# Attention scores of the token-order units in two full-height passes, with the units in another order

## The chip, the cores and the metric

The kernel runs on one core of one Trainium2 chip. The time is the device time of one launch in microseconds (us). The kernel before took 852.31 us, the median of 3 runs (850.77 to 853.92). A core has engines that each work through a queue of their own in order and wait for each other by semaphores: TensorE (PE: matrix products and transposes; weight loads are shown apart as PEld), VectorE (DVE), ScalarE (ACT), GpSimd (POOL) and SyncE (SP), which issues the DMAs here.

## The reference

One layer with 512 tokens, model width 1024, heads of 64. All inputs are float32.

```
hn   = rms_norm(x, ln_g);  proj = hn @ w_in
A    = block-sparse causal attention, 8 heads (with 512 tokens: causal over all keys)
B    = three groups of 8 heads, (window, dilation) = (128,1), (512,4), (2048,16),
       outputs mixed by their softmax denominators
C    = sliding window of 128, 8 query heads on 2 key heads, learned sinks
       (all: per-head rms_norm of q and k, relative-position bias, softmax)
br   = [A * silu(ga), B * silu(gb), C * silu(gc)] @ w_branch   (per branch)
out  = x + (sum over branches of sigmoid(gates) * br) @ w_out
```

## The kernel before, in words

A float32 value v is kept as two tiles, hi (v rounded to the type fp32r) and lo = v - hi. A product of two such values is written as three matmuls that add into one PSUM tile: hi·hi, hi·lo, lo·hi. The normalised input is held transposed as `xhi`, `xlo`.

**Units.** The attention work is cut into ten units, each half (4 heads) of one kind. Kind A is mixer A. Kinds W, R, Z are the three groups of mixer B. Kind C is mixer C. A, W and C work on the tokens in their order (`natural_attention`). R and Z work on residue classes of the token number modulo 4 (`residue_attention`). The order is A0 W0 R0 Z0 A1 W1 R1 Z1 C0 C1.

**Projection** (`project`). Per unit and per 128-token tile t, 24 matmuls (8 slices of the contraction, three passes) make 512 columns of q and k in the PSUM tile `pj`, and 24 more make 256 columns of v. Then per tile: ACT copies q and k to `qn` and squares them, DVE sums, POOL takes the power -1/2, DVE multiplies, PE transposes two head pairs of q and two of k (L420), ACT writes the hi part with the norm's gain and DVE the lo part (L430, L431). Two heads share a tile: the first in partitions 0 to 63, the second in 64 to 127. `qn` comes from a pool tag of 3 buffers.

**Scores** (`natural_attention`). For A and W a head's score of one query tile is made by `mm3` (L436, L437, L438) from 64 partitions: qhi·khi, qhi·klo, qlo·khi. Its width is 256 columns, for A 384 and 512 in the last two query tiles. For C the queries are already stacked: `stack_queries` (L342 to L349) makes for each head a tile with the hi part in partitions 0 to 63 and the lo part in 64 to 127, and the keys stand twice, so that L471 on 128 partitions gives (qhi + qlo)·khi and L472 on 64 partitions gives qhi·klo. Behind the scores: DVE adds the bias and takes the row minimum (L447), ACT takes the exponential (L448, with a read of the accumulator), PE transposes (L485), ACT and DVE write hi and lo of the transposed probabilities (`pthi`, `ptlo`), PE multiplies by v (L510). The residue units have their own loop: scores in plain float32 on 64 partitions (L535), transposes (L546), PV products by `mm3`, and copies of the result (L563).

**End of a unit** (`spread`). Per-row factors are brought to all 64 channels of a head by a product with a 0/1 matrix `emat` from 64 partitions (tile `pb`, L590).

**What sets the order.** The program is written unit by unit, and a scheduler then sets a fixed order on each engine by its own timing model, within the limits of data, buffers and explicit `issue_after` edges. `RATION` names the units during whose attention the next unit's projection is handed out piece by piece (A0, W0, W1, C0, C1). Elsewhere the scheduler may still pull projections of the next unit into an attention, as far as their buffers are free. The tags of q and k (`qhi`, `qlo`, `khi`, `klo`) have two buffers each. After the attention come gates, branch products and the output projection.

## Time and profile before

| | |
|---|---|
| median of 3 runs | 852.31 us (850.77 to 853.92) |
| the profiled execution, its own time | 849.95 us |
| its span, first to last instruction | 848.2 us |
| PE, PEld, DVE, ACT, POOL busy | 97%, 78%, 51%, 49%, 20% |
| mean granted TensorE clock | 0.989 |

The profile is that of one execution. The end of a matmul is modelled and overlaps the next one, so that busy shares of PE run high: the distance from one start to the next is the better price of a matmul. A matmul of 512 columns is shown as 128x512, and the partitions it contracts over stand ahead as 128*128 (contracted * output).

### The profile page before, as it was taken

How to read it: one execution, taken by the hardware profiler on the slowest of the kernel's cores; microseconds unless marked ns; L12 is line 12 of the kernel's file. 1: busy time of each engine (PE TensorE's matmuls, PEld its weight loads, DVE VectorE, ACT ScalarE, POOL GpSimd, SP SyncE). 2: the span in 40 equal slices, each digit the busy share in tenths (PEclk: the TensorE clock that was granted, in tenths of full speed). 3: DMA queues.
4: the chain of work that ended last, by engine and by line, in shares of the span. 5: the costliest groups of instructions: out<-in, count | busy, mean ns of one | idle time of the engine just before them, and what ended most of it. 6: DMA issues, size and time to landing. Idle time of an engine off the chain costs nothing.

```text
span 848.2 us, 11663 instructions
## 1 busy us (share of the span) xinstructions
PE 823.3 (97%) x4295; PEld 664.4 (78%) x4295; DVE 429.1 (51%) x981; ACT 412.8 (49%) x913; POOL 170.1 (20%) x113
## 2 busy tenths in 40 slices
PE   7999999999998999989999899999999999999998
PEld 5888887788877688868787777777888888888886
DVE  6746553645465567245555485645243733332612
ACT  5535553748577356256576845654344333222310
POOL 4333011122212321111131160103131310110200
PEclk9999999999999999999999899999999999999999
DMA  8445233251332042413332121503432431531302
GB/s 267 135 128 139 63 100 106 68 169 43 95 106 76 22 134 84 147 58 100 118 105 80 39 57 38 146 23 99 150 100 76 148 100 51 198 100 50 124 1 100
DMA packets 60605, 83.57 MB, mean 99 GB/s; under 512 B 4835, under 2 KB 40803, under 8 KB 60548
## 3 DMA queue, kind: packets, MB, share of 16 engines
q1 hardware_dynamic: 60548, 82.83, 31.4%
q8 instruction: 34, 0.56, 0.3%
q14 instruction: 23, 0.19, 0.1%
HBM read 74.36 MB, written 8.45 MB: 98 GB/s over the span
## 4 chain that ended last, share of the span: by engine, by line
PE 88%; ACT 5%; DVE 3%; issue 1%; DMA 1%; POOL 1%; DVEq 0%; SPq 0%; POOLq 0%; ACTq 0%
PE pj L363 12%; PE pj L364 11%; PE pj L365 11%; PE pj L266 8%; PE pj L268 8%; PE pj L267 8%; PE acc L856 5%; PE po L510 4%; PE tr L485 3%; PE po L830 3%; PE po L831 3%; PE po L832 3%; PE sc L436 2%; ACT lg L448 2%; PE tr L420 2%
## 5 line engine op out<-in xcount | busy, mean ns | idle before, releaser
L363 PE MATMUL pj<-whi,xhi 128*128 128x512 f32 (+1 forms) x576 | 204.0, 354 | 1.3 <-ACT xhi L130 0.7
L364 PE MATMUL pj<-wlo,xhi 128*128 128x512 f32 (+1 forms) x576 | 198.0, 344 | 0.0
L365 PE MATMUL pj<-whi,xlo 128*128 128x512 f32 (+1 forms) x576 | 196.6, 341 | 0.0
L135 DVE TENSOR_TENSOR wlo<-w,whi 128x1024 fp32r<-128x1024 f32 x82 | 109.1, 1338 | 113.6 <-ACT whi L130 112.7
L130 ACT CAST whi<-w 128x1024 fp32r<-128x1024 f32 x108 | 112.9, 1051 | 61.7 <-PE po L831 31.6
L135 POOL TENSOR_TENSOR wlo<-w,whi 128x1024 fp32r<-128x1024 f32 x28 | 68.1, 2432 | 309.7 <-ACT whi L130 309.6
L363 PEld LDWEIGHTS pj<-whi,xhi 128*128 128x128 f32 x576 | 109.5, 190 | 19.0 <-issue 2.5
L365 PEld LDWEIGHTS pj<-whi,xlo 128*128 128x128 f32 x576 | 109.2, 190 | 13.4 <-issue 1.3
L364 PEld LDWEIGHTS pj<-wlo,xhi 128*128 128x128 f32 x576 | 109.5, 190 | 12.1 <-issue 1.0
L266 PE MATMUL pj<-xhi,whi 128*128 128x512 f32 x288 | 115.4, 401 | 0.0
L268 PE MATMUL pj<-xhi,wlo 128*128 128x512 f32 x288 | 114.2, 397 | 0.0
L267 PE MATMUL pj<-xlo,whi 128*128 128x512 f32 x288 | 113.6, 394 | 0.0
L141 POOL TENSOR_TENSOR rr<-rv,mhalf 128x8 f32<-128x8 f32 (+2 forms) x40 | 65.1, 1629 | 231.2 <-DVE rv L139 216.7
L130 ACT CAST pthi<-tr 128x128 fp32r<-128x128 f32 (+3 forms) x112 | 44.2, 399 | 42.7 <-PE tr L485 37.5
L268 PEld LDWEIGHTS pj<-xhi,wlo 128*128 128x128 f32 x288 | 54.4, 189 | 12.0 <-issue 0.5
L266 PEld LDWEIGHTS pj<-xhi,whi 128*128 128x128 f32 x288 | 54.5, 189 | 11.6 <-issue 0.2
L267 PEld LDWEIGHTS pj<-xlo,whi 128*128 128x128 f32 x288 | 54.5, 189 | 11.3 <-issue 0.2
L135 DVE TENSOR_TENSOR ptlo<-tr,pthi 128x128 fp32r<-128x128 f32 (+3 forms) x112 | 50.8, 458 | 22.5 <-ACT pthi L130 20.2
L447 DVE CUSTOM_DVE_ANT_0 lg<-sc,bt 128x128 f32<-128x128 f32 (+3 forms) x128 | 41.9, 361 | 39.1 <-PE tr L485 29.5
L379 DVE TENSOR_REDUCE ss<-sq 128x8 f32<-128x512 f32 (+2 forms) x40 | 25.7, 643 | 47.9 <-ACT sq L377 47.5
L448 ACT ACTIVATE lg<-lg,sm 128x128 f32<-128x128 f32 (+1 forms) x96 | 40.2, 420 | 15.4 <-DVE sm L447 15.2
L448 ACT ACTIVATE lg<-lg,sl 128x128 f32<-128x128 f32 (+2 forms) x64 | 33.5, 523 | 26.9 <-DVE sl L447 26.6
(178 smaller groups left out, 1252.6 us busy)
## 6 DMA issues: line engine op xcount, KB each, us to landing
w<-in_w_in SPq DMA_DIRECT2D x54, 512.0 KB, 4.1
w<-in_w_in SPq DMA_DIRECT2D x72, 256.0 KB, 3.1
w<-in_w_branch SPq DMA_DIRECT2D x12, 512.0 KB, 3.4
vscr<-vn SPq DMA_DIRECT2D x16, 256.0 KB, 2.6
w<-in_w_out SPq DMA_DIRECT2D x8, 512.0 KB, 4.5
xt<-in_x SPq DMA_DIRECT2D x4, 512.0 KB, 6.5
bt<-scr SPq DMA_DIRECT2D x8, 256.0 KB, 3.1
bt<-scr SPq DMA_DIRECT2D x16, 128.0 KB, 3.0
```

The costliest lines, as they stand in the source:

```text
L130: A.copy(dst, src)
L135: eng.tensor_tensor(dst, src, hi.bitcast(F32), ALU.subtract)
L141: G.tensor_tensor(r, v, mhalf[:, :n], ALU.pow)
L266: T.matmul(psum, a, xhi[:, k, :], start=(k == 0), stop=False)
L267: T.matmul(psum, a, xlo[:, k, :], start=False, stop=False)
L268: T.matmul(psum, wlo(k)[:, c : c + 128], xhi[:, k, :], start=False, stop=(k == KT - 1))
L363: T.matmul(pj[:, :ncol], xh, whi(k), start=(k == 0), stop=False)
L364: T.matmul(pj[:, :ncol], xh, wlo(k), start=False, stop=False)
L365: T.matmul(pj[:, :ncol], xl, whi(k), start=False, stop=(k == KT - 1))
L447: V.tensor_tensor_reduce(lg, sc, bt, 1.0, init, ALU.add, ALU.min, mcol)
L448: last_exp[0] = A.activation(lg, lg, AF.Exp, bias=mcol, scale=-1.0, accum_out=lcol)
L856: T.matmul(acc[t * 2 + e], part[k // 2][:, k % 2, tsl], wo[q](k)[:, es], start=(k == 0 and q == 0 and part is mhi), stop=(k == KT - 1 and ...
```

## The change

Keys and queries of A and W are now stacked as those of C were: per head, 128 partitions with the query's hi part over its lo part, and the key twice. A score of A, W or C is two matmuls on 128 partitions, with the same stationary queries: one on the keys' hi tile, one on their lo tile. It now holds lo·lo as well. A key tile per head needs twice the memory, so `kh`, `kl` and the stacked queries `qs0`, `qs1` have one buffer each, and the residue units' `qf`, `kf` one each of their own. The units alternate: A0 R0 W0 Z0 A1 R1 W1 Z1 C0 C1. In `project`, the keys are normalised into a doubled tile `kd` and the queries go through `stack_queries`. `qn`, `kd` and the stack `qs` share the tag `qn` of 3 buffers. `spread` uses 128 partitions throughout (`emat` has zeros below), and goes group by group. The gains of the queries are folded into those of the keys (`gqk`).

```
-UNITS = ("A0", "W0", "R0", "Z0", "A1", "W1", "R1", "Z1", "C0", "C1")
+UNITS = ("A0", "R0", "W0", "Z0", "A1", "R1", "W1", "Z1", "C0", "C1")
...
-    for g in range(4):
+    for g in range(2):
         for h in range(8):
             em[32 * g + h, h * 64 : (h + 1) * 64] = 1.0
...
-        qkv = top.enter_context(tc.tile_pool(name="qkv", bufs=2))
+        qkv = top.enter_context(tc.tile_pool(name="qkv", bufs=1))
...
-            def pair_tile(nm):
-                return (
-                    qkv.tile([128, 2, S], F32R, name=nm + "hi", tag=nm + "hi"),
-                    qkv.tile([128, 2, S], F32R, name=nm + "lo", tag=nm + "lo"),
-                )
+            def stack_tiles(tags):
+
+                return tuple(qkv.tile([128, 2, S], F32R, name="qst", tag=tag) for tag in tags)
+
+            def key_tiles():
+
+                return tuple(qkv.tile([128, 4, S], F32R, name=tag, tag=tag) for tag in ("kh", "kl"))
 
             def full_tile(nm):
-                return (qkv.tile([128, 2, S], F32, name=nm + "f", tag=nm + "hi"),)
+                return (qkv.tile([128, 2, S], F32, name=nm, tag=nm),)
...
-                        if nh > nq:
+                        if pieces[-1][0] == "S":
+                            kd = qkv.tile([128, 512], F32, name="kd", tag="qn", bufs=3)
+                            V.tensor_tensor(
+                                kd.rearrange("p (h i d) -> p h i d", i=2, d=64),
+                                q3[:, nq:nh].unsqueeze(2).broadcast_to([128, 4, 2, 64]),
+                                r[:, nq:nh].unsqueeze(2).unsqueeze(3).broadcast_to([128, 4, 2, 64]), ALU.mult,
+                            )
+                        if pieces[1:] and pieces[1][0] == "K":
...
-                            for p in range(npair):
-                                T.transpose(tr[:, p], qn[:, o + p * 128 : o + p * 128 + 128], rev if ty == "q" else ident)
-                            g = {"q": gq, "k": gn, "K": gqk}[ty][:, gc : gc + 1]
+                            if ty == "S":
+                                npair = 4
+                                for h in range(4):
+                                    T.transpose(tr[:, h], kd[:, h * 128 : (h + 1) * 128], ident)
+                            else:
+                                for p in range(npair):
+                                    T.transpose(tr[:, p], qn[:, o + p * 128 : o + p * 128 + 128], rev if ty == "q" else ident)
+                            g = {"q": gq, "k": gn, "K": gqk, "S": gqk}[ty][:, gc : gc + 1]
...
-                qh, ql, kh, kl, vh, vl = u
+                qa, qb, kh, kl, vh, vl = u
...
-                        if kind == "C":
-                            qc = (qh, ql)[p]
-                            T.matmul(sc[:, :wm], qc[:, e, qs], kh[:, hf, ks], start=True, stop=False)
-                            pe = T.matmul(sc[:, :wm], qc[0:64, e, qs], kl[0:64, hf, ks], start=False, stop=True)
-                        else:
-                            pe = mm3(sc[:, :wm], qh[rows, p, qs], ql[rows, p, qs], kh[rows, p, ks], kl[rows, p, ks], True, True)
+
+                        qc = (qa, qb)[p][:, e, qs]
+                        kk = hf if kind == "C" else j
+                        T.matmul(sc[:, :wm], qc, kh[:, kk, ks], start=True, stop=False)
+                        pe = T.matmul(sc[:, :wm], qc, kl[:, kk, ks], start=False, stop=True)
...
-                wst = []
-                for g0 in range(0, ng, 2):
-                    n = 64 * min(2, ng - g0)
+
+                for g in range(ng):
                     tr = ps.tile([128, NT, 128], F32R, name="trs", tag="po")
                     for t in range(NT):
-                        T.transpose(tr[:n, t], ws[:, t, 64 * g0 : 64 * g0 + n], order)
+                        T.transpose(tr[:, t], ws[:, t, 64 * g : 64 * g + 128], order)
...
-                        es = emat[rows, (hf * 2 + p) * 128 : (hf * 2 + p + 1) * 128]
-                        T.matmul(pb, es, wst[g // 2][rows, :], start=True, stop=True)
+                        c = (hf * 2 + p) * 128
+                        T.matmul(pb, emat[:, c : c + 128], wt, start=True, stop=True)
                         use(p, g, pb)
...
-                    mk_ = full_tile if kind in "RZ" else pair_tile
-                    q, k, v = mk_("q"), mk_("k"), v_tile()
+                    if kind in "RZ":
+                        q, k, v = full_tile("qf"), full_tile("kf"), v_tile()
+                        pqk = [("q", q, 256, gc), ("k", k, 256, gc + 1)]
+                    else:
+                        q, k, v = stack_tiles(("qs0", "qs1")), key_tiles(), v_tile()
+                        pqk = [("s", q, 256, gc), ("S", k, 256, gc + 1)]
```

The other edits rename buffers of the start, the gates and the end to the new tags, and give pools an explicit number of buffers.

How the order on PE changes, at two places. First the scores in the attention of A0. In the kernel before, L436 to L438 are the three score passes, L363 to L365 the projection of the next unit, L485 the transposes of the probabilities:

```order
L436 MATMUL sc<-khi,qhi 128x256
L437 MATMUL sc<-klo,qhi 128x256
L438 MATMUL sc<-khi,qlo 128x256
L363 MATMUL pj<-whi,xhi 128x256
L364 MATMUL pj<-wlo,xhi 128x256
```

The same engine and unit in the changed kernel, where L496 and L497 are the two passes and L508 the transposes of the probabilities:

```order
L508 MATMUL tr<-idr,lg 128x128 x3
L496 MATMUL sc<-kh,qst 128x384
L497 MATMUL sc<-kl,qst 128x384
L508 MATMUL tr<-idr,lg 128x128 x5
L496 MATMUL sc<-kh,qst 128x512
L497 MATMUL sc<-kl,qst 128x512
```

Three matmuls per score became two, with one stationary tile, and no projection matmul stands between these scores and transposes. Second, PE inside the attention of the residue unit R0. In the kernel before, L535 are its scores, L546 its transposes, L510 the last PV products of the unit ahead (W0), L363 to L365 the projection of the next unit (Z0):

```order
L510 MATMUL po<-pthi,vlo 128x256
L510 MATMUL po<-ptlo,vlo 128x256
L546 MATMUL tr<-idr,lg 128x128 x7
L535 MATMUL sc<-kf,qf 128x128 x6
L364 MATMUL pj<-wlo,xhi 128x512
L365 MATMUL pj<-whi,xlo 128x512
L363 MATMUL pj<-whi,xhi 128x512
```

In the changed kernel, where L558 are R0's scores, L569 its transposes, L533 the last PV products of A0, L603 transposes for the products with `emat`:

```order
L569 MATMUL tr<-idr,lg 128x128 x3
L533 MATMUL po<-pthi,vlo 128x512
L603 MATMUL trs<-revr,ws 128x128 x4
L569 MATMUL tr<-idr,lg 128x128
L558 MATMUL sc<-kf,qf 128x128 x8
L533 MATMUL po<-ptlo,vlo 128x512
L533 MATMUL po<-pthi,vlo 128x384
L533 MATMUL po<-ptlo,vlo 128x384
L533 MATMUL po<-pthi,vlo 128x256
L533 MATMUL po<-ptlo,vlo 128x256
```

The projection matmuls that stood between R0's own work are gone from this place. They stand later, between R0's last products and the scores of W0. Counted over the whole order of PE, from a residue unit's first score to its last PV product: R0 has 63 projection matmuls of 512 columns before and 5 now, R1 63 and 24, Z1 24 and 4. Z0 has 10 of 512 columns and 44 of 256 before, and 3 of 512 now. The last PV products (8) of the unit ahead and 4 to 6 more transposes now stand inside Z0 and Z1. R0 has 15 such PV products and 29 transposes, where it had 8 and 22, and 2 products with `emat` with 4 transposes of their own. R1 has none of these PV products and 20 transposes, where it had 8 and 22.

## Rows read from the trace of the kernel before

**Rows 1.** The page's first part: busy time, share of the span and number of instructions of each engine.

```profile
PE 823.3 (97%) x4295; PEld 664.4 (78%) x4295; DVE 429.1 (51%) x981; ACT 412.8 (49%) x913; POOL 170.1 (20%) x113
```

**Rows 2.** The page's fourth part: the chain that ended last, shares of the span by engine.

```profile
PE 88%; ACT 5%; DVE 3%; issue 1%; DMA 1%; POOL 1%; DVEq 0%; SPq 0%; POOLq 0%; ACTq 0%
```

**Rows 3.** A stretch of 20 us in the gates, where PE does nothing but matmuls of 512 columns on 128 partitions. Columns: window, length, then busy us and number of instructions of each engine, PE's granted clock, DMA share, GB/s.

```profile
600.00:620.00 20.00, 20.00 (x89) 16.41 (x88) 1.49 (x2) 4.56 (x7) 2.41 (x1) 1.00 0.34 119
```

**Rows 4.** PE in order of time around a score of 256 columns in the attention of A0. Columns: start, us, engine, line, operation, out<-in, contracted*output, shape.

```profile
96.61 0.27 PE L510 MATMUL po<-ptlo,vhi 128*128 128x256 f32 x1
96.82 0.38 PE L436 MATMUL sc<-khi,qhi 64*128 64x256 f32 x1
97.04 0.28 PE L437 MATMUL sc<-klo,qhi 64*128 64x256 f32 x1
97.16 0.28 PE L438 MATMUL sc<-khi,qlo 64*128 64x256 f32 x1
97.36 0.38 PE L363 MATMUL pj<-whi,xhi 128*128 128x256 f32 x1
97.59 0.28 PE L364 MATMUL pj<-wlo,xhi 128*128 128x256 f32 x1
97.70 0.29 PE L365 MATMUL pj<-whi,xlo 128*128 128x256 f32 x1
```

**Rows 5.** Groups by line and shape on PE. Columns: line, engine, operation, out<-in, shapes, count, busy us and mean ns of one, idle before.

```profile
L436 PE MATMUL sc<-khi,qhi 64*128 64x256 f32 x48 | 17.4, 366 | 0.9 <-DVE sm L447 0.8
L436 PE MATMUL sc<-khi,qhi 64*128 64x512 f32 x8 | 3.8, 478 | 0.5 <-DVE sl L447 0.5
L436 PE MATMUL sc<-khi,qhi 64*128 64x384 f32 x8 | 3.5, 440 | 0.0
L590 PE MATMUL pb<-wst,emat 64*128 64x512 f32 x20 | 9.4, 497 | 0.6 <-DVE wst L583 0.6
```

**Rows 6.** PE in order of time around a score in the attention of C0. Columns as in rows 4.

```profile
509.89 0.28 PE L510 MATMUL po<-ptlo,vhi 128*128 128x256 f32 x1
510.01 0.28 PE L471 MATMUL sc<-khi,qhi 128*128 128x256 f32 x1
510.22 0.38 PE L472 MATMUL sc<-klo,qhi 64*128 64x256 f32 x1
510.53 0.33 PE L485 MATMUL tr<-idr,lg 128*128 128x128 f32 x1
510.62 0.36 PE L510 MATMUL po<-pthi,vhi 128*128 128x256 f32 x1
```

**Rows 7.** PE in order of time around two products with `emat` at the end of A0. Columns as in rows 4.

```profile
134.14 0.40 PE L364 MATMUL pj<-wlo,xhi 128*128 128x512 f32 x1
134.46 0.50 PE L590 MATMUL pb<-wst,emat 64*128 64x512 f32 x1
134.89 0.49 PE L365 MATMUL pj<-whi,xlo 128*128 128x512 f32 x1
135.32 0.50 PE L590 MATMUL pb<-wst,emat 64*128 64x512 f32 x1
135.75 0.50 PE L363 MATMUL pj<-whi,xhi 128*128 128x512 f32 x1
136.09 0.40 PE L364 MATMUL pj<-wlo,xhi 128*128 128x512 f32 x1
```

**Rows 8.** Transposes of q and k: groups by shape on PE (float32 as in L420, fp32r as in L346), columns as in rows 5.

```profile
L420 PE MATMUL tr<-idr,qn 128*128 128x128 f32 x136 | 23.8, 278 | 2.3 <-DVE qn L390 1.2 <-DVE klo L431 1.1
...
L346 PE MATMUL tr<-revr,qs 128*128 128x128 f32 x32 | 4.3, 260 | 0.0
```

**Rows 9.** Four of these in a run, in order of time, columns as in rows 4 (the us are from the first one's start to the last one's end).

```profile
228.21 0.60 PE L420 MATMUL tr<-idr,qn 128*128 128x128 f32 x4
...
484.84 0.51 PE L346 MATMUL tr<-revr,qs 128*128 128x128 f32 x4
```

**Rows 10.** The attentions of the residue units, from the first score to the last product or copy: R0, Z0, R1, Z1. Columns as in rows 3.

```profile
188.40:215.20 26.80, 26.80 (x159) 22.33 (x159) 15.98 (x49) 21.07 (x56) 6.34 (x4) 1.00 0.22 61
233.90:254.30 20.40, 18.33 (x130) 16.04 (x130) 12.68 (x43) 15.22 (x48) 3.14 (x2) 0.92 0.38 110
409.70:436.60 26.90, 26.90 (x159) 22.39 (x159) 16.04 (x49) 21.13 (x56) 6.38 (x4) 1.00 0.22 60
452.00:474.20 22.20, 18.45 (x104) 14.27 (x104) 13.06 (x48) 16.88 (x49) 3.68 (x2) 0.86 0.33 100
```

**Rows 11.** Groups by line and shape on ACT that make up a residue unit's attention, columns as in rows 5.

```profile
L448 ACT ACTIVATE lg<-lg,sm 128x128 f32<-128x128 f32 x72 | 28.1, 391 | 12.9 <-DVE sm L447 12.8
...
L563 ACT COPY oraw<-po 64x256 f32<-64x256 f32 x32 | 19.6, 614 | 4.0 <-PE po L438 3.8
...
L448 ACT ACTIVATION_READ_ACCUMULATOR lg<-lg,sm 128x1 f32 x96 | 18.0, 188 | 0.0
...
L130 ACT CAST pthi<-tr 128x512 fp32r<-128x512 f32 x24 | 13.8, 587 | 4.0 <-PE tr L485 2.7 <-PE tr L546 1.2
```

**Rows 12.** Groups by line and shape on DVE: norm of q and k, lo part of the keys, the two steps of `stack_queries`. Columns as in rows 5.

```profile
L390 DVE TENSOR_TENSOR qn<-qn,rr 128x512 f32<-128x512 f32 x32 | 28.2, 881 | 23.4 <-POOL rr L141 23.4
...
L431 DVE SCALAR_TENSOR_TENSOR klo<-tr,gn,khi 128x256 fp32r<-128x256 f32 x16 | 7.6, 477 | 8.2 <-ACT khi L430 8.1
...
L343 DVE TENSOR_TENSOR qs<-qn,qs 128x256 fp32r<-128x256 f32 x4 | 1.7, 419 | 0.1
...
L342 DVE CAST qs<-qn 128x256 fp32r<-128x256 f32 x4 | 1.2, 290 | 1.5 <-PE tr L346 1.4
```

More of the change, by code (lines that the diff above doesn't have):

```diff
@@ L178, in start_x @@
         def start_x():
-            lrow = qkv.tile([1, D], F32, name="lrow", tag="vhi")
+            lrow = qkv.tile([1, D], F32, name="lrow", tag="vhi", bufs=2)
             nc.sync.dma_start(lrow, ln_g)
@@ L189, in load_x @@
             def load_x(t):
-                xt = qkv.tile([128, D], F32, name="xt", tag=("qhi", "qlo")[t % 2])
+                xt = qkv.tile([128, D], F32, name="xt", tag=("qs0", "qs1", "qf", "kf")[t])
                 nc.sync.dma_start(xt, x2[t * 128 : (t + 1) * 128, :])
@@ L255, in start_small @@
             V.tensor_scalar(gq, gn, -0.125, None, ALU.mult)
-            V.tensor_tensor(gqk[:, 5:6], gq[:, 4:5], gn[:, 5:6], ALU.mult)
+            for i in (1, 3, 5):
+                V.tensor_tensor(gqk[:, i : i + 1], gq[:, i - 1 : i], gn[:, i : i + 1], ALU.mult)
             sk = qkv.tile([128, 8], F32, name="sk", bufs=1)
@@ L269, in gate_cols @@
                 yield
[L271 removed]
+        tags_raw = [None, None, "vhi", "vlo", "qs0", "qs1"]
         raws = {}
@@ L297, in raw_columns @@
                 jw[n + 1] = job_load(n + 1)
+                if n == 0:
+                    both = qkv.tile([128, 4, S], F32, name="graw", tag="kl")
                 for hf in range(2):
-                    raw = qkv.tile([128, 2, S], F32, name="graw", tag=tags_raw[n * 2 + hf])
+                    tag = tags_raw[n * 2 + hf]
+                    if tag is None:
+                        raw = both[:, hf * 2 : hf * 2 + 2]
+                    else:
+                        raw = qkv.tile([128, 2, S], F32, name="graw", tag=tag, bufs=2 if tag[0] == "v" else 1)
                     for p in range(2):
@@ L313, in body @@
             identr = at.tile([128, 128], F32R, name="identr", bufs=1)
-            ws = at.tile([128, NT, 192], F32R, name="ws", bufs=1)
-            for c in range(0, 192, 32):
+            ws = at.tile([128, NT, 256], F32R, name="ws", bufs=1)
+            for c in range(0, 256, 32):
                 G.tensor_copy(ws[:, :, c : c + 32], zer.rearrange("p (t c) -> p t c", t=NT))
@@ L367, in project @@
                             yield
-                    n = sum(p[2] for p in pieces if p[0] in "qskK")
+                    n = sum(p[2] for p in pieces if p[0] in "qskKS")
                     nh = n // 64
@@ L377, in project @@
                         A.activation(sq[:, :n], qn[:, :n], AF.Square)
-                        ss = qkv.tile([128, 8], F32, name="ss", tag="ss")
+                        ss = qkv.tile([128, 8], F32, name="ss", tag="ss", bufs=2)
                         V.tensor_reduce(
@@ L642, in unit_project @@
                 if kind == "C":
-                    q = pair_tile("q")
                     if hf == 0:
-                        cstate["k"], cstate["v"] = pair_tile("k"), v_tile()
+                        q = stack_tiles(("qs0", "qs1"))
+                        both = qkv.tile([128, 4, S], F32R, name="kc", tag="kh")
+                        cstate["k"], cstate["v"] = (both[:, 0:2], both[:, 2:4]), v_tile()
                         pieces = [("s", q, 256, 4), ("K", cstate["k"], 128, 5), ("V", cstate["v"], 128, 0)]
@@ L648, in unit_project @@
                     else:
+                        q = stack_tiles(("qf", "kf"))
                         pieces = [("s", q, 256, 4)]
-                        qb = qkv.tile([128, NT, 256], F32, name="qb", tag="khi")
+                        qb = qkv.tile([128, NT, 256], F32, name="qb", tag="vhi", bufs=2)
                     uq[ui] = q + cstate["k"] + cstate["v"]
@@ L794, in silu @@
                         V.tensor_tensor(o[:, p], sg, o[:, p], ALU.mult)
-                    parts = []
-                    for _ in range(2):
-                        tag = slots.pop(0)
-                        if tag:
-                            parts.append(qkv.tile([128, 2, S], F32R, name="bp", tag=tag))
-                        else:
-                            parts.append(gp.tile([128, 2, S], F32R, name="bp", tag="bp", bufs=1))
+                    tags = slots.pop(0)
+                    if isinstance(tags, str):
+                        both = qkv.tile([128, 4, S], F32R, name="bp", tag=tags)
+                        parts = [both[:, 0:2], both[:, 2:4]]
+                    else:
+                        parts = []
+                        for tag in tags:
+                            pool, tag, nb = (qkv, tag, 2 if tag[0] == "v" else 1) if tag else (gp, "bp", 1)
+                            parts.append(pool.tile([128, 2, S], F32R, name="bp", tag=tag, bufs=nb))
                     split_hi(parts[0], o)
@@ L867, in body @@
         for t in range(NT):
-            xr = qkv.tile([128, D], F32, name="xr", tag=("qhi", "qlo")[t % 2])
+            xr = qkv.tile([128, D], F32, name="xr", tag=("qs1", "oraw")[t % 2], bufs=(1, 4)[t % 2])
             nc.sync.dma_start(xr, x2[t * 128 : (t + 1) * 128, :])
```

26 lines of the change are left out of this document (11 added, 15 removed).

## The prediction

> **What bounds the kernel now.** I read the page's busy shares first: PE is busy 97% of the span, no other engine over 51% [rows 1]. Then the chain that ended last: 88% of it is PE [rows 2]. A busy PE need not be PE at its peak, so I looked at the distance between starts, in order of time. In the gates 89 matmuls of 512 columns take 20 us, 0.226 us each [rows 3], and in a plain run one of 256 columns takes half of that, 0.115 us (97.59 to 97.70) [rows 4]. Around the scores the distances are longer. The reader is to see in rows 4 that a start comes late wherever the number of contracted partitions goes from 128 to 64 or back: 0.21 us from L510 to L436, 0.22 from L436 to L437, 0.20 from L438 to L363, 0.23 from L363 to L364, but only 0.12 between L437 and L438, which both stand on 64. So PE is the limit, and a good part of its time is lost at these changes. Last I looked at the four residue attentions, the places where PE has least to do [rows 10].
>
> **What goes: the row changes and one pass.** One score of 256 columns, with its neighbours, reaches from 96.61 to 97.59, 0.98 us. Less the two neighbours (2 x 0.115) it costs 0.75 us. Three plain passes would be 0.345, so 0.405 us is the price of the two changes. The changed kernel needs two plain passes and no change: 0.23 us. It saves 0.52 us. For 384 and 512 columns the pass that goes is longer, so they save 0.405 + 0.17 = 0.575 and 0.405 + 0.226 = 0.63 us. With the counts of [rows 5]: 48 x 0.52 + 8 x 0.575 + 8 x 0.63 = 25.0 + 4.6 + 5.0 = 34.6 us.
> The scores of C have the same trouble in their second pass. From 509.89 to 510.62 there are 0.73 us [rows 6]. Less the L510 (0.115) and the transpose (0.107, below), the two passes cost 0.51, against 0.23 afterwards: 0.28 us saved. Where a matmul follows in place of a transpose, the way back to 128 partitions costs about 0.1 more, as at L363 in rows 4, so up to 0.40. I take 0.33, nearer to the row itself, for 8 heads x 4 tiles = 32 scores: 10.6 us.
> The products with `emat` go from 64 to 128 partitions too. From 134.14 to 136.09 five matmuls of 512 columns stand, two of them these [rows 7]: 1.95 - 5 x 0.226 = 0.82 us, 0.41 each, x20 [rows 5]: 8.2 us.
> Sum saved on PE: 53.4 us.
>
> **What comes on PE.** 16 projected tiles (4 units of A and W, 4 tiles each). Keys need 4 float32 transposes for 2: four in a run take 0.60 us [rows 9] and one 0.278 [rows 8], so a further one costs (0.60 - 0.28)/3 = 0.107. 32 x 0.107 = 3.4 us. Queries need 4 fp32r transposes for 2 float32 ones. One costs (0.51 - 0.26)/3 = 0.083 [rows 8, 9]: 64 x 0.083 - 32 x 0.107 = 1.9 us. `spread` of mixer B has three groups of 4 transposes where it had two, twice: 8 x 0.083 = 0.7 us. Together 6.0 us. Net on PE: -47.4 us.
>
> **What comes on the other engines.** DVE per tile: `kd` is a new multiplication of 512 columns (0.88 us) while the old one shrinks from 512 to 256 (0.42, as its like in L343), the queries' 0.48 becomes 0.29 + 0.42, and the keys' lo part doubles (0.48 to between 0.69 and 0.95, the lower end if a fixed part is in it) [rows 12]. That is about 1.0 us x 16 = 16 us on an engine that is busy 51% [rows 1]. ACT gets up to 12 us in the same way. I cost both at nothing: the next tile's 24 projection matmuls (24 x 0.226 = 5.4 us) cover them. If that cover is gone, 1.0 us of each of 16 tiles shows: 16 us. A tile now takes all three `qn` buffers (`qn`, `kd`, `qs`), so the next tile's copy out of PSUM waits for this one's queries. I put 1 us down for this, between 0 and 16, near the end at which the pure stretches of projection ahead of W0 and W1 lie.
>
> **What the new order uncovers.** This is the main cost. Before, the residue attentions R0 and R1 ran under full PE (26.8 of 26.8 us busy), while Z0 and Z1, with less projection among them, took 20.4 and 22.2 us with 2.1 and 3.8 us of them idle [rows 10]. The unit's softmax and copies on ACT set that floor: 16 x (0.391 + 0.188) + 4 x 0.587 + 8 x 0.614 = 16.5 us of ACT alone [rows 11], with projection work of the next unit beside it. In the order of the changed kernel the single-buffered keys hold the next unit's projection back (the counts stand with the change).
> R0: 58 matmuls of 512 fewer, -13.1 us. 7 more PV products, 7 transposes, 2 products with `emat` and their transposes, +2.3. PE's work falls from 26.8 to 16.0 us, under a floor of 21.3 (the mean of Z0 and Z1): 5.3 us of waiting.
> R1: 39 fewer (-8.8), 8 PV products and 2 transposes fewer (-1.1): 26.9 to 17.0, waiting 4.3.
> Z0: 7 matmuls of 512 and 44 of 256 fewer (-6.6), 8 PV products and 6 transposes more (+1.6): it already waits, so all 5.0 show.
> Z1: 20 fewer (-4.5), +1.3: 3.2 show.
> Sum 17.8 us. Bounds: if the floor is ACT's bare 16.5 us, R0 waits 0.5 and R1 nothing, and Z0 and Z1 come out at 16.5, 3.9 and 5.7 us shorter than now: -9. If all four take the 26.8 us of R0 before, 10.8 + 9.8 + 6.4 + 4.6 = +32. I take the floor of Z0 and Z1, since they are the rows with little projection among them.
> In the attentions of W0 and W1 some scores stand with little projection between them. There the time that PE lost at row changes hid a part of the wait for exponentials. I put 3 us down for this, between 0 and 5 (10 of the 32 scores of W stand so, x 0.52).
>
> **The sum.** Against the profiled execution: 849.95 - 47.4 + 1 + 17.8 + 3 = 824.4 us. The median of the runs stands 2.4 us above that execution, so 826.8: I predict 827 us.
>
> **A rule that speaks against it.** In rows 4 the step from L437 to L438 on 64 partitions, 0.12 us, is that of 128 partitions. The Trainium skill, TensorE: Matmul & The Clock Gate, table of "Why this matters for your kernels", says the same: a matmul with a short contraction takes as long as a full one, and the gain lies in running two on distinct row groups at once. By it alone only the third pass goes, and the time would be that of the second rival below. The Trainium skill, TensorEngine Tiling (Array Packing), Key Properties, says that a change of the tiling mode drains TensorE. By that rule, the trace agrees: the late starts of rows 4, 6 and 7 stand at the changes and not inside a run on 64 partitions.
>
> **Rivals.**
> 1. The waits stay where they are: the scheduler's order happens to cover the residue units as before, the floor being ACT's bare work. For it: DVE and ACT are half idle [rows 1]. Against it: 63 projection matmuls in R0 became 5. Time: 849.95 - 47.4 + about 2 (+2.4) = 807.
> 2. Slower: only the pass goes, not the price at its sides. If the 0.1 us per step belong to the load of a new stationary tile for a score (small groups with new weights each) and not to the change of rows, the stacked passes pay them too. Place: all 64 + 32 scores and the 20 products. Then only 48 x 0.115 + 8 x 0.17 + 8 x 0.226 = 8.7 us go, 6.0 come, and the uncovered waits remain: 849.95 - 2.7 + 21.8 (+2.4) = 871. It decides as soon as less than 28 us of the 53.4 are real (6.0 + 21.8 come on). Against it: L471 with a new stationary tile on 128 partitions starts 0.12 us after L510, without any delay [rows 6].
> 3. The waits take nearly all: all four residue attentions come out as long as R0 before (+32), and W's softmax shows in full (+5): 849.95 - 47.4 + 32 + 5 + 1 (+2.4) = 843. For it: PE fell to a granted clock of 0.92 and 0.86 in the attentions in which it idled [rows 10], and an idle R0 and R1 would add to that. Against it: what is uncovered there is short work for ACT, which is busy 15.2 of 20.4 us in Z0.
>
> **How the numbers follow.** Forecast (815 to 838) 0.70, rival 1 0.11, rival 3 0.13, rival 2 0.06. About 0.5% of 852.3 is what a measurement of this kernel can tell from no change, 4.3 us. Faster by more than that is below 848: the forecast, rival 1, most of rival 3, together 0.91. Rival 3 with a little more on top is no change, 0.03. Rival 2 is slower, 0.06. The range reaches from rival 1 to rival 3: 808 to 845.
>
> **What would show it right or wrong.** In the profile after: the two passes L496, L497 start 0.115 us apart at 256 columns, and the matmul before and after them has no late start (else rival 2). The products with `emat` are 0.226 us from the next start. C's second pass has no gap. PE's busy time falls by far more than the span, and the idle time of PE grows in the attentions of R0 and Z0 most, with ACT's exponentials and pthi as releasers and a granted clock below 1 there. The gates and the rest behind 570 us keep their length. I am wrong if PE's idle time at the residue units doesn't grow (the time is then near 807) or if the transposes of W0's keys and queries wait for DVE tile after tile (the `qn` buffers).

## The result: slower by 0.8%

The changed kernel takes 859.45 us, the median of 4 runs (856.78 to 860.17), beside 852.26 us for the kernel before on the same chip (4 runs, 850.77 to 853.92). The ratio is 1.0078, 95% interval 1.005 to 1.0107. The forecast was 827 us, faster. It was wrong on the side as well as in size.

The page's first part, of the kernel after. To compare with [rows 1]:

```profile
PE 805.2 (94%) x4303; PEld 670.6 (78%) x4303; DVE 443.5 (52%) x1017; ACT 418.6 (49%) x929; POOL 168.7 (20%) x115
```

PE is busy for 18 us less, and yet the span grew from 848.2 to 857.7 us. DVE got 14.4 us more (16 were forecast) and ACT 5.8 (up to 12). So what counts is where PE stands still.

PE in order of time around two scores in the attention of A0 after the change (columns as in rows 4):

```profile
92.34 0.39 PE L377 MATMUL pj<-whi,xlo 128*128 128x512 f32 x1
92.57 0.28 PE L496 MATMUL sc<-kh,qst 128*128 128x256 f32 x1
92.69 0.28 PE L497 MATMUL sc<-kl,qst 128*128 128x256 f32 x1
92.81 0.39 PE L375 MATMUL pj<-whi,xhi 128*128 128x512 f32 x1
93.04 0.39 PE L376 MATMUL pj<-wlo,xhi 128*128 128x512 f32 x1
93.27 0.40 PE L377 MATMUL pj<-whi,xlo 128*128 128x512 f32 x1
93.51 0.34 PE L496 MATMUL sc<-kh,qst 128*128 128x384 f32 x1
```

The late starts of [rows 4] are gone: 0.12 us from L496 to L497 and on to the projection. A score of 256 columns costs the 0.23 us that were forecast.

The four residue attentions after, from the first score to the last copy (columns as in rows 3, in the order of [rows 10] but with R0 ahead of W0):

```profile
133.70:158.50 24.80, 19.05 (x116) 15.24 (x115) 16.68 (x55) 18.70 (x56) 1.94 (x2) 0.93 0.46 125
249.40:270.40 21.00, 17.47 (x102) 14.44 (x102) 13.14 (x45) 16.68 (x51) 1.61 (x1) 0.84 0.37 107
361.70:384.80 23.10, 18.45 (x107) 14.06 (x106) 13.27 (x45) 18.85 (x52) 3.99 (x2) 0.93 0.40 109
476.90:497.40 20.50, 16.62 (x103) 13.31 (x102) 12.96 (x45) 16.72 (x51) 2.18 (x1) 0.92 0.38 110
```

PE is idle there for 5.8, 3.5, 4.7 and 3.9 us, where it was 0, 2.1, 0 and 3.8, and the granted clock is below 1 in all four. The four lengths add up to 89.4 us. The forecast had 85.2: its floor of 21.3 us for R0 and R1, and the lengths of before for Z0 and Z1.

To see the rest I added up the distances between the starts of PE, less the plain time of each instruction (0.231 us per 512 columns, 0.109 a transpose). A remainder above 0.25 us counts as a wait (0.35 where the number of rows changes), a smaller one as a row change where the rows differ and as rest elsewhere. Half of the time at the lower clock level stands apart. All such sums here are of one execution each. In us:

| | half clock | waits | row changes | rest |
|---|---|---|---|---|
| before | 7.1 | 27.9 | 33.5 | 23.1 |
| after | 15.1 | 61.0 | 6.8 | 18.4 |

The row changes did go. The waits took back more than they gave. This sum doesn't say which part of the change makes the waits; the runs do.

### The profile page after: what moved, and what is told of

Its sections match the earlier page's. It is cut to its first block, busy times and chain, and to the rows that moved or that the text cites. A ratio compares the mean times of both kernels' runs of the same rounds, so it can differ in the third digit from the quotient of the medians.

```text
span 857.7 us, 11746 instructions
## 1 busy us (share of the span) xinstructions
PE 805.2 (94%) x4303; PEld 670.6 (78%) x4303; DVE 443.5 (52%) x1017; ACT 418.6 (49%) x929; POOL 168.7 (20%) x115
## 5 line engine op out<-in xcount | busy, mean ns | idle before, releaser
L132 ACT CAST whi<-w 128x1024 fp32r<-128x1024 f32 x108 | 113.2, 1050 | 63.3 <-PE po L858 31.7
L375 PEld LDWEIGHTS pj<-whi,xhi 128*128 128x128 f32 x576 | 111.0, 193 | 23.1 <-issue 7.3
L143 POOL TENSOR_TENSOR rr<-rv,mhalf 128x8 f32<-128x8 f32 (+2 forms) x40 | 62.2, 1560 | 314.6 <-DVE rv L141 310.3
L270 PEld LDWEIGHTS pj<-xlo,whi 128*128 128x128 f32 x288 | 54.2, 188 | 10.6
L849 ACT ACTIVATE gsg<-pj 128x512 f32<-128x512 f32 x24 | 14.3, 596 | 65.6 <-PE pj L271 65.6
```

What stands on the lines that cost most here:

```text
L132: A.copy(dst, src)
L143: G.tensor_tensor(r, v, mhalf[:, :n], ALU.pow)
L270: T.matmul(psum, a, xlo[:, k, :], start=False, stop=False)
L375: T.matmul(pj[:, :ncol], xh, whi(k), start=(k == 0), stop=False)
```

## The experiments

Theory 1: the row changes cost real time, and the new order, the single buffers or the stacked projection give it back as waits. Theory 2: the late starts were worth nothing. Each kernel was timed against the kernel before on its own chip (851.6 to 853.1 us); differences are to that median. The ratios in brackets, with their 95% intervals, are not made from the medians and differ from them by up to 0.23%, so differences of about 2 us between two runs are not told apart.

### The parts one by one

**C and the emat products alone** (`rows_c_pb`), on the kernel before:

```
-  T.matmul(sc[:, :wm], qc[0:64, e, qs], kl[0:64, hf, ks], ...)
+  T.matmul(sc[:, :wm], qc[:, e, qs], kl[:, hf, ks], ...)
...
-  T.matmul(pb, es, wst[g // 2][rows, :], start=True, stop=True)
+  T.matmul(pb, emat[:, c : c + 128], wt, start=True, stop=True)
```

> The kernel before with only C's second score pass and the products with emat on 128 partitions; unit order, buffers and A/W scores unchanged. Theory 1 (the row changes cost real time on the path, and the changed kernel lost it again to waits of its order and buffers): 10.6 + 8.2 = 18.8 us less by my prices, about 833 us. Theory 2 (the late starts at row changes only stand beside waits, so their removal gives nothing anywhere): 848 to 853 us.

844.17 us, 7.6 less (ratio 0.9911, 0.9886 to 0.9937). That the late starts are worth nothing is refuted, but 11 of the 18.8 us are missing.

**A/W scores alone** (`aw_128_old_buffers`):

```
-  pe = mm3(sc[:, :wm], qh[rows, p, qs], ql[rows, p, qs], kh[rows, p, ks], kl[rows, p, ks], True, True)
+  T.matmul(sc[:, :wm], qh[:, p, qs], kh[:, p, ks], start=True, stop=False)
+  pe = T.matmul(sc[:, :wm], qh[:, p, qs], kl[:, p, ks], start=False, stop=True)
```

> The kernel before with A/W scores as two passes on all 128 partitions of the old tiles: a score then sums the two heads that share a tile and leaves out the pass lo x hi, so the output is not the reference's; order, buffers, transposes and DVE work are those of before. Theory 1: the whole 34.6 us of my term go, about 818 us (815 to 826 if a few attentions of W wait). Theory 2: only the pass goes, 8.7 us, 843 us, or nothing. Theory 3 (PE's saved time in A and W turns into waits for exponentials in whatever order): above 835 us.

828.98 us, 22.8 less (0.9721, 0.9691 to 0.9752). Two thirds of the term are there, and the time lies between the 826 and the 835 us of the two theories.

**The order alone** (`order_only`): the line of `UNITS`, with all buffers double.

> The kernel before with only the alternating order of units; double buffers and three-pass scores stay. Theory 1a (the order alone uncovers the residue units): 15 to 25 us more, 867 to 877 us. Theory 1b (the single buffers of the stacked keys and queries uncover them, the order is harmless where every tag has two buffers): 848 to 856 us.

870.04 us, 18.3 more (1.0208, 1.017 to 1.0246). The order does it without single buffers. R0's attention in this kernel (columns as in rows 3):

```profile
139.30:161.00 21.70, 19.95 (x107) 16.16 (x107) 13.94 (x54) 14.65 (x50) 0.42 (x1) 0.76 0.41 116
```

The granted clock was 0.76 there. In [rows 10] R0 ran at 1.00. PE is idle there for only 1.8 us, and in the other three attentions for 2.4, 2.3 and 3.3. By the sum over the starts, this execution has about 11 us more of waits than before, most of them outside these attentions, and about 9 us more of half clock.

**All three together** (`aw_c_pb_order_double`).

> The kernel before with all three at once, A/W scores in two passes on 128 partitions (two heads summed, lo x hi left out, as in aw_128_old_buffers), C and emat products on 128 partitions, and the alternating order; what is still missing of the change are the stacked projection (kd, stacked queries, more transposes) and the single buffers. If the three effects add: 851.8 - 22.8 - 7.6 + 18.3 = 840 us (835 to 845), and the remaining 19 us of the changed kernel belong to stacked projection and single buffers. If the order's waits eat what the cheaper scores save (they are worth less where PE waits): 850 us or more.

840.43 us, 11.2 less (0.9864, 0.9845 to 0.9883). The three differences add to -12.1. Within the noise the effects add, so the order doesn't eat the cheaper scores. What is still missing of the change must cost about 19 us.

**The changed kernel without the stacked projection** (`after_plain_projection`):

```
-  pqk = [("s", q, 256, gc), ("S", k, 256, gc + 1)]
+  pqk = [("q", q, 256, gc), ("k", k, 256, gc + 1)]
...
-  kk = hf if kind == "C" else j
+  kk = hf if kind == "C" else j // 2
```

> The changed kernel with q and k of A/W projected as in the kernel before (one normalising product, two transposes each, hi and lo tiles; half of each doubled key tile stays unwritten and is not read, the scores sum heads, output not the reference's); single buffers and order as changed. If the stacked projection (6 us of transposes, the kd and qs steps on DVE, all three qn buffers per tile) costs the remaining 19 us: 838 to 845 us. If the single buffers do: 852 to 857 us, only the transposes gone.

838.21 us, 13.4 less (0.9842, 0.9819 to 0.9865). Against the run before this is -2.2 for the single buffers, with the smaller edits: they cost nothing. Against the changed kernel (7.2 more than before) it is 20.6 us for the stacked projection. That is the largest single loss.

The first scores of the residue units cut the profiled executions into stretches, and show where it arises (us; the lower three kernels are those of the next section):

| | to R0 | R0 to Z0 | Z0 to R1 | R1 to Z1 | Z1 to the end |
|---|---|---|---|---|---|
| `after_plain_projection` | 133.6 | 106.8 | 112.1 | 104.4 | 379.9 |
| the changed kernel | 133.7 | 115.7 | 112.3 | 115.2 | 380.8 |
| `after_lbufs3` | 138.3 | 117.9 | 112.3 | 115.1 | 380.6 |
| `after_qn5_lbufs3` | 136.9 | 111.5 | 116.5 | 110.0 | 379.0 |
| `after_qs_own_tag` | 130.6 | 113.2 | 134.0 | 106.4 | 395.0 |

Nearly all of the loss, 8.9 and 10.8 us, lies between R0 and Z0 and between R1 and Z1, where W0 and W1 are projected and used. A1's projection, between Z0 and R1, costs 0.2 us.

**A row-changing pass put back** (`after_third_pass`):

```
+  if kind != "C":
+      T.matmul(sc[:, :wm], qc[0:64], kh[0:64, kk, ks], start=True, stop=True)
   T.matmul(sc[:, :wm], qc, kh[:, kk, ks], start=True, stop=False)
```

> The changed kernel with an idle pass of 64 partitions ahead of each A/W score, whose sum the next pass overwrites: it brings back the row changes of A and W, 0.3 to 0.43 us x 64 = 22 us of PE time. If PE still bounds A's and W's attention in the changed kernel: 881 us. If PE waits there for exponentials and keys, about half is absorbed: 865 to 872 us.

881.41 us, 29.7 more than before, so 22.5 more than the changed kernel. A pass and its row changes cost there what `aw_128_old_buffers` saved by leaving them out (22.8). PE still bounds these attentions.

### What in the stacked projection costs

**Transposes alone** (`plain_projection_64_more`), on `after_plain_projection`. (An earlier run meant for this, `plain_projection_more_transposes`, held `after_plain_projection` itself and gave 838.45 us, as that did.)

```
   for p in range(npair):
+      if perm == "N" and ty in "qk":
+          T.transpose(tr[:, 2 + p], qn[:, o + p * 128 : o + p * 128 + 128], ident)
       T.transpose(tr[:, p], qn[:, o + p * 128 : o + p * 128 + 128], rev if ty == "q" else ident)
```

> after_plain_projection with two idle float32 transposes more for the q and two for the k of each projected tile of A and W, 64 in all. If the transposes cost what I priced (0.107 us each, 6.8 us): 843 to 847 us, and the other 14 us of the stacked projection are waits of its chain and its buffers. If they come where PE has the time: 838 to 841 us, and all of the 21 us are waits.

838.15 us (0.9801, 0.9766 to 0.9837): nothing more. They were executed; here are their group (L445, columns as in rows 5) and the span and granted clock, in the order without and with them:

```profile
L445 PE MATMUL tr<-idr,qn 128*128 128x128 f32 x64 | 15.5, 274 | 0.3 <-DVE qst L457 0.3
```

```profile
core 0: 836.8 us, clock 0.982
```

```profile
core 0: 836.7 us, clock 0.988
```

By the sum over the starts, 7.0 us of transposes came, 5.1 us of half clock and 2.6 us of waits went. So 64 transposes more do not make the 20.6 us by themselves; what stands around them must. It is not shown that they come free in the changed kernel too: against `after_plain_projection` its sum has the 7.0 us of transposes, about 11 us more of waits and about 1 us more of half clock.

**The qn buffers** (`after_qn5_lbufs3`, and `after_lbufs3` as its control): `tag="qn", bufs=3` becomes `bufs=5`, and `LBUFS = 4` becomes 3.

> The changed kernel with five buffers for the tag qn in place of three; the memory comes from the weight staging (LBUFS 3 in place of 4). If the third projected tile of q and k waits for qn buffers that kd and qs hold, so that the V projection of W0 and W1 can't run in the residue attentions: the added waits of the stacked projection go, 8 to 12 us less, 848 to 852 us. If the kd and qs steps on DVE or the extra transposes themselves are the cost: 857 to 861 us.

> The changed kernel with LBUFS 3 alone, to see what the smaller weight staging costs by itself. Either theory: 858 to 862 us.

The control takes 866.59 us, 14.4 more than before (1.0191, 1.0161 to 1.022). With five buffers it is 853.87, 1.7 more (1.0026, 1.0009 to 1.0043). With the smaller staging, the two buffers are worth 12.7 us. That it costs 7 us I had not expected, and its cause stays open. (In the control the transposes of the stacked queries wait 7.8 us for DVE, in the changed kernel 1.4, with five buffers 2.7.) As the control has these 7 us, part of the 12.7 may be a loss that the staging brought: against the changed kernel itself the five buffers are 5.5 us better, and a little slower than the 848 to 852 us expected. The stretches above tell more. Between R0 and Z0, and R1 and Z1, the five buffers take 6.4 and 5.1 us less than the control (4.2 and 5.2 less than the changed kernel); between Z0 and R1 they take 4.2 more than either. The projection matmuls inside R0's attention show what the buffers do. First the changed kernel (window 133.7 to 158), then five buffers (136.9 to 162), then the plain projection (133.6 to 158), columns as in rows 5:

```profile
L376 PE MATMUL pj<-wlo,xhi 128*128 128x512 f32 x2 | 0.9, 450 | 0.0
L377 PE MATMUL pj<-whi,xlo 128*128 128x512 f32 x2 | 0.8, 394 | 0.0
L375 PE MATMUL pj<-whi,xhi 128*128 128x512 f32 x1 | 0.4, 393 | 0.0
```

```profile
L377 PE MATMUL pj<-whi,xlo 128*128 128x256 f32 x12 | 3.4, 286 | 0.0
...
L376 PE MATMUL pj<-wlo,xhi 128*128 128x256 f32 x11 | 3.1, 285 | 0.0
L375 PE MATMUL pj<-whi,xhi 128*128 128x256 f32 x11 | 3.1, 279 | 0.0
```

```profile
L376 PE MATMUL pj<-wlo,xhi 128*128 128x256 f32 x11 | 3.2, 295 | 0.0
L375 PE MATMUL pj<-whi,xhi 128*128 128x256 f32 x11 | 3.1, 279 | 0.0
L377 PE MATMUL pj<-whi,xlo 128*128 128x256 f32 x11 | 3.0, 277 | 0.0
```

With five buffers, or without `kd` and `qs`, the V projection of W0 (256 columns) runs inside R0's attention. In the changed kernel none of it does, and in the control none either. R1's attention is alike: 48 such matmuls with five buffers and with the plain projection, none in the changed kernel. PE there in order of time, at the end of that attention (columns as in rows 4, the idle time and its releaser in brackets):

```profile
157.10 0.60 PE L441 MATMUL tr<-idr,kd 128*128 128x128 f32 x4
158.64 0.51 PE L357 MATMUL tr<-revr,qs 128*128 128x128 f32 x4 [0.94 <-ACT oraw L586]
159.78 0.39 PE L375 MATMUL pj<-whi,xhi 128*128 128x256 f32 x1 [0.63 <-ACT qn L387]
160.00 0.29 PE L376 MATMUL pj<-wlo,xhi 128*128 128x256 f32 x1
```

And ACT in the same stretch:

```profile
157.30 1.23 ACT L586 COPY oraw<-po 64x256 f32<-64x256 f32 x2
158.56 0.69 ACT L454 ACTIVATE kh<-tr,gqk 128x512 fp32r<-128x512 f32 x1
159.15 0.58 ACT L387 COPY qn<-pj 128x512 f32<-128x512 f32 x1
```

In the order that was set with three buffers, the next tile's copy to `qn` (L387) comes behind the transposes that empty `kd` and `qs` (L441, L357). The copy frees a `pj` tile, and only then does the V projection begin, at 159.78, 1.25 us behind the attention's last copy.

**qs in buffers of its own** (`after_qs_own_tag`):

```
-  qs = qkv.tile([128, 4, 128], F32R, name="qs", tag="qn", bufs=3)
+  qs = at.tile([128, 4, 128], F32R, name="qs", tag="wst", bufs=2)
```

> The changed kernel with the stacked queries qs in the two buffers of the tag wst in place of the tag qn, so that a projected tile takes two of the three qn buffers. If tiles wait for qn buffers: 3 to 10 us less, 849 to 856 us. If not: 858 to 861 us.

879.29 us, 27.7 more than before (1.0323, 1.0303 to 1.0343), a miss. The tag `wst` is the one that `spread` uses, so A1's first queries stand behind the end of mixer B (PE, columns as above):

```profile
283.45 1.22 PE L609 MATMUL pb<-wst,emat 128*128 128x512 f32 x2 [0.78 <-DVE wst L605]
285.11 0.75 PE L357 MATMUL tr<-revr,qs 128*128 128x128 f32 x4 [0.43 <-DVE qs L354]
```

A borrowed buffer brings its own queue. The stretches tell the two effects apart: the loss, 21.7 and 14.2 us against the changed kernel, lies behind Z0 and behind Z1, where mixer B ends. From R0 to Z0 and from R1 to Z1 this kernel is 2.5 and 8.8 us shorter than the changed one, with the full staging, which fits a tile that holds one `qn` buffer less.

### Can a ration mend the order?

`after_even_ration` hands out the next unit's projection in every attention, `after_qn5_residue_ration` only in R0, Z0 and R1 (an entry per unit in `RATION`, and a step of the residue attention after its scores, each transposed tile and each product).

> The changed kernel with the next unit's projection handed out evenly over the attention of every unit up to Z1 (RATION for all, 4 steps ahead, then 1.7 per step in A and W, 6 in R and Z, 2.8 in Z1). If the added waits and the half clock (33 + 8 us by my count over the starts on PE) come from projection that the scheduler put ahead of the residue attentions, where it is missing: most of them go, 825 to 835 us. If they come from the chain of the stacked projection itself, or from ACT's throughput: 850 to 860 us.

> after_qn5_lbufs3 with RATION also for R0, Z0 and R1 (0 steps ahead, 9 per step): the projection of the next A or W unit may not be taken into the attention ahead and stands inside the residue attention. If what the order costs (18.3 us in order_only) comes from projection that the scheduler takes too early: 10 to 18 us below after_qn5_lbufs3. If the attentions of A0 and W0 then lack that work: the same or more.

961.31 us and 903.51 us: 109.7 and 51.3 more than before. My theory that the scheduler takes the projection too early is not borne out; held back, it does more harm. The end of a unit in the first of them shows how, in order of time:

```profile
267.62 0.40 PE L377 MATMUL pj<-whi,xlo 128*128 128x512 f32 x1
268.06 0.58 ACT L387 COPY qn<-pj 128x512 f32<-128x512 f32 x1
270.76 0.68 DVE L391 TENSOR_REDUCE ss<-sq 128x8 f32<-128x512 f32 x1
271.79 1.64 POOL L143 TENSOR_TENSOR rr<-rv,mhalf 128x8 f32<-128x8 f32 x1 [6.56 <-DVE rv L141]
273.46 0.69 DVE L409 TENSOR_TENSOR qn<-qn,rr 128x512 f32<-128x512 f32 x1 [1.81 <-POOL rr L143]
274.30 1.08 PE L444 MATMUL tr<-idr,qn 128*128 128x128 f32 x4 [6.28 <-DVE qn L409]
```

From the last projection matmul of a tile to its transposes the chain over ACT, DVE and POOL takes 6.7 us, some 1.5 of them behind the split of a weight tile on ACT and DVE. With nothing else placed there, PE stands still for 6.28 of them. This is the price of one tile whose cover is gone. Such waits of the transposes for DVE are most of the loss in both kernels. In the second they are 23.6 and 19.8 us. Here are the two largest in the first, and then the same two in the changed kernel (us in all, how often, the longest):

```profile
PE tr L357 <- DVE qs L354: 48.2, 12, 5.3
PE tr L444 <- DVE qn L409: 37.3, 14, 6.3
```

```profile
PE tr L444 <- DVE qn L409: 4.8, 5, 1.6
...
PE tr L357 <- DVE qs L354: 1.4, 2, 0.9
```

### The sizes of the PE terms

**A/W without row changes, nothing else** (`aw_three_pass_128`): `mm3` keeps its three passes, on `[:, p, ...]` instead of `[rows, p, ...]`. Every engine has the same instructions as before, in the same order but for five of PE's records at two scores.

> The kernel before with its three A/W score passes on all 128 partitions of the old tiles (two heads summed, output not the reference's): the instructions of every engine stand in the same order as before, and only the row changes of these scores are gone. If each of the 64 scores pays the 0.405 us that I read at one place, and PE is the bound there: 26 us less, 826 us. If the mean price is less or waits take part of it: 834 to 842 us, and the trace shows which: late starts that stay without a releaser, or waits with one.

832.17 us, 19.4 less (0.9776, 0.9755 to 0.9798). The place of [rows 4] in this kernel:

```profile
97.10 0.28 PE L365 MATMUL pj<-whi,xlo 128*128 128x256 f32 x1
97.22 0.29 PE L436 MATMUL sc<-khi,qhi 128*128 128x256 f32 x1
97.34 0.28 PE L437 MATMUL sc<-klo,qhi 128*128 128x256 f32 x1
97.46 0.28 PE L438 MATMUL sc<-khi,qlo 128*128 128x256 f32 x1
97.58 0.28 PE L363 MATMUL pj<-whi,xhi 128*128 128x256 f32 x1
97.70 0.28 PE L364 MATMUL pj<-wlo,xhi 128*128 128x256 f32 x1
```

From the start ahead of the score to the second one behind it 0.60 us pass (97.10 to 97.70), where it was 0.98 (96.61 to 97.59). Less five plain distances of 0.115 us, 0.03 is left of the 0.405. The price at the place was right. Summed over the 62 places at which such scores stand, the late starts were 25.9 us before, as priced, and 4.9 are left, 3.3 of them beside transposes, where a wait stays. So 21.0 us went there, and the kernel gained 19.4, 0.30 us a score instead of 0.405. The waits over the whole of PE stay as they were (27.7 us by the sum above). The Trainium skill, TensorEngine Tiling (Array Packing), Key Properties, says that a change of the tiling mode drains TensorE. This run agrees with that: nothing but the changes of rows was taken out, and the late starts beside them went. The third pass, whose removal I priced at 8.7 us, gives only 22.8 - 19.4 = 3.4, of which some 2 us are noise. By the sum over the starts of `aw_128_old_buffers` its 8.7 us did go from PE, and about 4 us of waits came in their place.

**C alone** (`before_c_only`, the first line of the edit of `rows_c_pb`), **emat's rows alone** (`emat_rows_only`, the products on 128 partitions with the groups in pairs as before) and **both with a later fill** (`c_and_emat_late_fill`, here against `rows_c_pb`):

```
-  for c in range(0, 256, 32):
+  for c in range(0, 192, 32):
       G.tensor_copy(ws[:, :, c : c + 32], ...)
...
   start_bias()
+  G.tensor_copy(ws[:, :, 192:256], emat[:, 256:512].rearrange("p (t c) -> p t c", t=NT))
```

> The kernel before with only C's second score pass on 128 partitions. If the C term was right (10.6 us) and the 7.6 us of rows_c_pb are that less a cost in the emat part: 839 to 842 us. If the C term is 7.6 us or less and the emat part gives nothing: 844 to 846 us.

> The kernel before with the products with emat on 128 partitions of the old tiles (other groups' rows are added in, output not the reference's), ws as wide as before and the groups in pairs as before, so that the order changes at a few places only. If the price of 0.41 us x 20 was right: 844 us. If these products stand where PE waits anyway: 850 to 853 us.

> rows_c_pb with the last 64 columns of ws filled after the projection of A0 instead of two zero fills ahead of it on POOL. If the emat edit lost its gain at the start: 836 to 840 us. If not: 842 to 845 us.

C alone: 842.18 us, 10.0 less by the medians, 8.3 by the ratio (0.9903, 0.9876 to 0.9931); the term was 10.6. Emat's rows alone: 847.68, 3.9 less (0.9952, 0.9934 to 0.9971); the term was 8.2. Both with the later fill: 839.88, 11.7 less (0.9863, 0.9848 to 0.9877), against 7.6 in `rows_c_pb`. So the emat edit as it stands gains nothing. It costs 2.4 us by the medians (7.6 against 10.0) and 0.7 by the ratios, which is not clear of noise. With two POOL fills fewer at the start the kernel is 4.1 us faster (11.7 against 7.6), which is clear of noise. `rows_c_pb` loses this at the start: R0's first score comes at 194.0 us there, at 188.5 with C alone and at 189.3 with the later fill. The second unit's projection waits:

```profile
54.52 0.38 PE L363 MATMUL pj<-whi,xhi 128*128 128x256 f32 x1 [3.25 <-DVE vlo L135]
```

With the later fill the longest wait for `vlo` there is 0.5 us. `c_and_emat_late_fill` leaves nothing of the computation out and is the fastest such kernel of this study, 1.4% faster than before.

## Why the prediction was wrong

The predicted change of -25.3 us (827 against 852.3) and the measured +7.2 differ by 32.5 us. Term by term, in us:

| step | forecast | measured | run |
|---|---|---|---|
| A/W scores, with 3 for W's softmax | -31.6 | -22.8 | aw_128_old_buffers |
| C's second pass | -10.6 | -10.0 | before_c_only |
| emat products | -8.2 | +2.4 (not clear of 0) | rows_c_pb less before_c_only |
| order and buffers | +17.8 | +18.3 - 2.2 | order_only, after_plain_projection |
| transposes 6, qn buffers 1, DVE and ACT 0 | +7.0 | +20.6 | after less after_plain_projection |

The measured column adds to 6.3, and 0.9 more is what the three parts lack in adding up (-11.2 against -12.1): 7.2. The forecast missed most at the stacked projection (13.6 us), then at emat (10.6) and at A/W (8.8).

**The step that failed most** is "I cost both at nothing: the next tile's 24 projection matmuls (24 x 0.226 = 5.4 us) cover them", with the 1 us "near the end at which the pure stretches of projection ahead of W0 and W1 lie". With the transposes, 7 us were forecast for the stacked projection, and 20.6 measured. It priced the added instructions by their busy time and looked for cover beside the tile. At least a part of the loss lies elsewhere: `kd` and `qs` hold the three `qn` buffers until the transposes, so W's V projection, which covers the residue attention where it can run, can't start. The upper ends I had noted (16 for the chain, 16 for the buffers) hold the 20.6 us. I took the lower ones, and the range didn't reach there. Two more buffers give 12.7 us with the smaller staging, 5.5 against the changed kernel itself. The rest, 8 to 15 us (the transposes, the DVE steps, the longer chain), I did not try apart. `kd` itself is short: its 16 multiplications take 0.69 us each, not the 0.88 of the forecast. My sign for this error, transposes waiting for DVE tile after tile, was the wrong place to look in the changed kernel: those of the queries wait 1.4 us in all (L357 above), and the matmul behind the transposes at 158.64 waits for ACT's copy to `qn`.

**Second, a size:** emat's 0.41 us each was read at one stretch in which both neighbours were projection matmuls. Over all 20, the rows gave 3.9 us instead of 8.2, and the edit's own cost at the start, about 4 us, took that.

**Third, a size:** A/W's 34.6 us. The row changes gave 19.4 of 25.9 and the third pass 3.4 of 8.7, where waits came in its place.

**A sum that was wrong:** the bounds of the order's term. For Z0 and Z1 they take only the change of length and leave out the 5.0 and 3.2 us of PE work that the term itself moves out of these attentions. With them the bounds are about -1 and +40 us instead of -9 and +32, and rival 3 stands at 851 instead of 843 us. The measured time is outside the range even so.

**What was right, and what was luck.** C's term is near. PE's idle time in R0 and R1 grew by 5.8 and 4.7 us, where 5.3 and 4.3 were forecast; in Z0 and Z1 by 1.4 and 0.1 instead of 5.0 and 3.2. That the order alone costs 18.3 us, where 17.8 were forecast, is in good part luck: nearly half of it is half clock, for which the sum had no term, and most of its waits lie outside these attentions. The reason I gave with it, "the single-buffered keys hold the next unit's projection back", was wrong: the order alone does it with double buffers, and the single ones cost nothing. The stationary tile's price (rival 2) is refuted by 92.57 to 92.81 above and by the same order without row changes. The time is on rival 2's side, slower, but not by its cause: the price of the row changes did go. Rival 3 came nearest as a mechanism: the waits take nearly all. It lacked the stacked projection.

## What to carry to other kernels

Price an added step by the buffers it holds and by what can then not be pulled forward, and not by its busy time alone: two buffers more were worth 12.7 us beside the smaller staging, and 7 us of transposes on PE cost nothing in the kernel in which they were tried. A late start read at one place can hold in the sum (25.9 us over 62 places) and the kernel still gain less (19.4); a kernel with the same instructions and only that cost removed tells how much. An agreement of two totals, like 17.8 and 18.3, wants a look at what the time consists of. Where several edits come together, measure them singly first: here two gains of 10 and 23 us were spent on an order and a projection that only one of them needed.

## What the runs showed of the hardware that I had not expected

64 additional transposes (7 us of PE) left the span at 836.7 us, and the mean granted clock rose from 0.982 to 0.988. Over all executions it is 0.980 to 0.985 in eight without them and 0.986 to 0.992 in four with them. By the sum over the starts, less half clock gave back 5.1 of the 7.0 us. And in `rows_c_pb` one DVE multiplication of 512 columns took 2.86 us beside a POOL instruction of 2.38 us, where its like takes 0.67 to 0.69 (columns as in rows 4):

```profile
39.46 2.38 POOL L135 TENSOR_TENSOR wlo<-w,whi 128x1024 fp32r<-128x1024 f32 x1
39.53 2.86 DVE L390 TENSOR_TENSOR qn<-qn,rr 128x512 f32<-128x512 f32 x1 [0.39 <-POOL rr L141]
48.29 0.67 DVE L390 TENSOR_TENSOR qn<-qn,rr 128x512 f32<-128x512 f32 x1
```

The two overlap from 39.53 to 41.84. The traces of all runs here bear this out. Of 496 such multiplications of 512 columns, 74 took 1.4 to 2.9 us, and each of these overlapped a POOL instruction of 128x1024 or on `oraw`. None of the 368 with no POOL instruction beside it took more than 0.70 us. Eight ran beside such a one for over 0.5 us and were not slowed, so an overlap alone is not enough; what else it takes stays open.
